# Two-layer decoder trunk: group norm, even units' scores and the mixed inputs of layer B placed anew between the products

## The chip, the cores and the metric

One core of one Trainium2 chip runs the kernel. The metric is the device time of one execution in microseconds (us), taken as the median of several runs.

## The reference

One inference step of a trunk of two layers, for a prompt of 256 tokens (with 16 meta tokens ahead, 272 positions) and 8 samples of one token. All is fp32. Layer A is RWKV-7 time mixing, layer B grouped-query attention over a window of 128 with sinks. Cut to what matters here:

```python
def rwkv7_step(S, inp):
    r, d, k, v, kk, b = inp
    sa = jnp.einsum('bhij,bhj->bhi', S, kk)
    S = S * d[:, :, None, :] - sa[..., None] * b[:, :, None, :] + v[..., None] * k[:, :, None, :]
    return S, jnp.einsum('bhij,bhj->bhi', S, r)
...
    rkvz = jnp.einsum('btpd,pde->btpe', xm[:, :, :4], w_rkvz)
...
    S_fin, y = lax.scan(rwkv7_step, S0.astype(f32), ...)
    y = (y - mean) * lax.rsqrt(var + GN_EPS) * gn_g + gn_b
    y = y + jnp.sum(r_h * k_h * r_k, axis=-1, keepdims=True) * v_h
    y = y.reshape(B, T, WIDTH) * jax.nn.silu(z)
    return y @ w_out, S_fin, xn[:, -1]
```

After layer A one shared key/value product `w_kv` is taken of the stream, and layer B's products `w_qz` and `w_o` follow. The weights of layer A's four input products have 2048 x 4096 entries each, `w_out` 4096 x 2048, `w_kv` 2048 x 1024.

## The kernel before

**Products.** Each fp32 weight tile is split into a high and a low half (`split`, L192: ACT casts `whi` at L195, DVE subtracts to `wlo` at L197), and each product is three matmuls per tile (`mm3`, L218 high by high, L219 high by low, L220 low by high) over 280 columns (the 272 positions and the 8 samples). `products()` cuts them into pieces of six such matmuls, and `self.pos` counts pieces.

**The recurrence between them.** `phase_a` calls `drive` (L608), which goes through the pieces in order. Ahead of each piece it lets a list of streams (Python generators) put in their small work, and each stream says with its `yield` for how many pieces it then sleeps and, if it likes, for which condition. PE runs all of this in the order in which it is written. The heads of layer A are worked in 16 units of 4 heads, `u`, two units to a call `o`:

- `prep(u)` makes the unit's inputs: two small gate products (`ps_l`), then a DMA that spreads the norms of the keys into `kk`, and on DVE the key times its norm (L898), two scans (L910) and more.
- `scores(u)` multiplies keys and queries inside chunks of 64 positions, in five steps: three groups of matmuls (`ps_sc`, L1017 and L1031; DVE reads them at L1024, L1025, L1037 and L1038, ACT at L1023 and L1036) and two groups of transposes (`ps_bk`). For an even unit every step takes both banks of the PSUM pool `pe`, which has two. The gaps between its steps are 8, 6, 6, 5, 4 pieces.
- `substitute(o)` inverts the triangles of 16 on DVE: a transpose to `NL` (L1069), 14 pairs of small operations (L1075, L1077), transposes to `TN` (L1081) and `TR` (L1082). `solve(o)` goes on with four groups of small matmuls on PE (`ps_so`, L1102, L1108, L1120, L1129), the first of them 24 or 27 pieces after the scores.
- `chain(o)` walks over five chunks: W (L1191), two pieces later X (L1205, L1208), three later G (L1214, L1217), five later the next W. It is written in `main()`, whose work has a higher priority in the scheduler of the other engines' instructions.
- `group_norm(o)` (L1255) normalises the result, 36 pieces later transposes it back in four groups of three transposes (L1275, `ps_yt`), three pieces apart, two groups to one double bank, and adds each to the bonus `vT` on DVE (L1276).
- `bo` (L954) is the product that makes the bonus, `vk` (L854) a copy on ACT of transposed values.

**Layer B's inputs.** Once the stream is done, `out_a` starts the `w_kv` product (`ps_kv`). `phase_b` then makes the 16 mixed inputs `bmx` of `w_qz` with `norm_mix`, an ACT operation (L1464, `bmh`) and a DVE operation (L1465, `bml`) each, all 16 written at one place.

## Time and profile before

| | us |
|---|---|
| median of 3 runs | 2120.92 |
| lowest, highest run | 2119.35, 2124.57 |
| the profiled execution | 2118.32 |
| its span in the trace | 2116.5 |
| PE busy in it | 2064.9 (98%) |
| DVE busy | 1697.8 (80%) |
| ACT busy | 1263.8 (60%) |
| the 16 DMA engines, mean busy share | 66.6% |

The profiled execution is 1.8 us longer than its span, and 2.6 us below the median of the runs. Busy times are of the span. The start of a PE row is the time from which to read (the ends of matmuls are modelled, and one overlaps the next), and PEclk is the share of full clock that TensorE was granted.

### The profile page before, as it was taken

Reading aid. Unit: us, or ns where it says so; the run is one execution under the profiler, and the core shown is the slowest. Engines: PE = TensorE matmul, PEld = TensorE weight load, DVE = VectorE, ACT = ScalarE, POOL = GpSimd, SP = SyncE. Lnnn points to the kernel's source line nnn. Section 1 sums busy time; section 2 is a strip of 40 time slices with the busy share of each in tenths; the row PEclk is TensorE's granted clock in tenths of the full one; section 3 lists DMA queues with packets and bytes.
Section 4 is the critical chain, followed back from the end, with each engine's and each line's share of the span. In section 5 each row is a group of like instructions: output and inputs, shape, how many; then the busy total and the mean of one; then the engine's idle time right before and its main releaser. Section 6 shows DMA issues by size and latency. Waiting matters only on the chain.

```text
span 2116.5 us, 55871 instructions
## 1 busy us (share of the span) xinstructions
PE 2064.9 (98%) x21420; PEld 1965.8 (93%) x21420; DVE 1697.8 (80%) x4112; ACT 1263.8 (60%) x2790; POOL 122.5 (6%) x188
## 2 busy tenths in 40 slices
PE   9999999899999999999999999999999999999997
PEld 7999899889899989899999999999999999999997
DVE  8867777687678878888888788997888888878885
ACT  3457766576766757767676445565565655544443
POOL 0011100001010010100100001100000000000000
PEclk9999999999999999999999999999999999999999
DMA  7898667658756876777657687757455444567774
GB/s 258 314 312 250 189 213 241 188 181 290 216 180 205 260 229 198 211 217 222 203 152 246 207 257 243 247 172 227 132 167 156 146 155 130 181 210 247 232 219 132
DMA packets 276356, 446.28 MB, mean 211 GB/s; under 512 B 54056, under 2 KB 97768, under 8 KB 275696
## 3 DMA queue, kind: packets, MB, share of 16 engines
q1 hardware_dynamic: 275656, 441.66, 66.6%
q8 instruction: 168, 2.75, 0.5%
q10 hardware_dynamic: 432, 1.05, 0.1%
q14 instruction: 100, 0.82, 0.1%
HBM read 381.69 MB, written 65.03 MB: 211 GB/s over the span
## 4 chain that ended last, share of the span: by engine, by line
PE 87%; DVE 5%; ACT 3%; DMA 3%; issue 2%; SPq 0%; POOL 0%; DVEq 0%; POOLq 0%; ACTq 0%
PE ps_z L218 6%; PE ps_z L219 6%; PE ps_z L220 6%; PE ps_k L218 3%; PE ps_ob L218 3%; PE ps_ob L220 3%; PE ps_v L218 3%; PE ps_ob L219 3%; PE ps_r L218 3%; PE ps_q L218 3%; PE ps_q L220 3%; PE ps_q L219 3%; PE ps_k L219 3%; PE ps_k L220 3%; PE ps_v L220 3%; PE ps_v L219 3%
## 5 line engine op out<-in xcount | busy, mean ns | idle before, releaser
L218 PE MATMUL ps_z<-mhlm,whi_z 128*128 128x280 f32 x512 | 158.6, 310 | 2.8 <-ACT sr L937 2.0
L219 PE MATMUL ps_z<-mhlm,whi_z 128*128 128x280 f32 x512 | 150.6, 294 | 0.0
L220 PE MATMUL ps_z<-mhlm,wlo_z 128*128 128x280 f32 x512 | 150.3, 294 | 0.0
L218 PE MATMUL ps_q<-bmh,whi_qb 128*128 128x264 f32 x512 | 150.0, 293 | 0.1
L218 PE MATMUL ps_z<-bmh,whi_zb 128*128 128x264 f32 x512 | 147.4, 288 | 0.0
L220 PE MATMUL ps_q<-bmh,wlo_qb 128*128 128x264 f32 x512 | 145.6, 284 | 0.6 <-DVE wlo_qb L197 0.6
L219 PE MATMUL ps_q<-bml,whi_qb 128*128 128x264 f32 x512 | 145.6, 284 | 0.0
L219 PE MATMUL ps_z<-bml,whi_zb 128*128 128x264 f32 x512 | 145.5, 284 | 0.0
L220 PE MATMUL ps_z<-bmh,wlo_zb 128*128 128x264 f32 x512 | 145.4, 284 | 0.0
L218 PE MATMUL ps_ob<-ghi,whi_ob 128*128 128x264 f32 x512 | 145.3, 285 | 0.0
L220 PE MATMUL ps_ob<-ghi,wlo_ob 128*128 128x264 f32 x512 | 144.6, 284 | 0.0
L219 PE MATMUL ps_ob<-glo,whi_ob 128*128 128x264 f32 x512 | 144.6, 283 | 0.0
L195 ACT CAST whi_ob<-raw_ob 128x512 fp32r<-128x512 f32 x128 | 79.1, 620 | 96.9 <-PE ps_ob L219 77.8
L195 ACT CAST whi_oa<-raw_oa 128x512 fp32r<-128x512 f32 x128 | 79.2, 620 | 88.0 <-PE ps_oa L219 30.6
L197 DVE TENSOR_TENSOR wlo_r<-raw_r,whi_r 128x512 fp32r<-128x512 f32 x128 | 87.8, 691 | 42.6 <-ACT whi_r L195 41.3
L218 PE MATMUL ps_v<-mhlm,whi_v 128*128 128x280 f32 x384 | 119.8, 312 | 0.4 <-ACT st L790 0.4
L218 PE MATMUL ps_k<-mhlm,whi_k 128*128 128x280 f32 x384 | 119.1, 310 | 1.0 <-ACT st L790 1.0
L195 ACT CAST whi_v<-raw_v 128x512 fp32r<-128x512 f32 x128 | 79.0, 619 | 65.8 <-PE ps_v L219 37.7
L197 DVE TENSOR_TENSOR wlo_v<-raw_v,whi_v 128x512 fp32r<-128x512 f32 x128 | 87.3, 687 | 36.9 <-ACT whi_v L195 35.6
L195 ACT CAST whi_zb<-raw_zb 128x512 fp32r<-128x512 f32 x128 | 78.2, 619 | 62.9 <-PE ps_z L219 38.5
L220 PE MATMUL ps_k<-mhlm,wlo_k 128*128 128x280 f32 x384 | 112.4, 293 | 2.1 <-issue 2.1
L219 PE MATMUL ps_v<-mhlm,whi_v 128*128 128x280 f32 x384 | 112.7, 293 | 0.0
(478 smaller groups left out, 7604.1 us busy)
## 6 DMA issues: line engine op xcount, KB each, us to landing
raw_k<-a_w_rkvz SPq DMA_DIRECT2D x128, 256.0 KB
raw_v<-a_w_rkvz SPq DMA_DIRECT2D x128, 256.0 KB
raw_r<-a_w_rkvz SPq DMA_DIRECT2D x128, 256.0 KB
raw_z<-a_w_rkvz SPq DMA_DIRECT2D x128, 256.0 KB
raw_oa<-a_w_out SPq DMA_DIRECT2D x128, 256.0 KB
raw_qb<-b_w_qz SPq DMA_DIRECT2D x128, 256.0 KB
raw_zb<-b_w_qz SPq DMA_DIRECT2D x128, 256.0 KB
raw_ob<-b_w_o SPq DMA_DIRECT2D x128, 256.0 KB
```

Of the source, the lines that this page charges most:

```text
L195: self.nc.scalar.copy(hi, src)
L197: return self.nc.vector.tensor_tensor(lo, src, hi.bitcast(F32), op=ALU.subtract)
L218: mm(ps, wh, xh, start=start, stop=False)
L219: mm(ps, wh, xl, start=False, stop=False)
L220: return mm(ps, wl, xh, start=False, stop=stop)
```

## The change

1. `drive` takes `main` ahead of the epilogues in each piece, and notes in `self.ran` the piece in which `main` stepped. `near(n)` is a condition that holds when `main` stepped in this same piece, or n pieces after it was set.
2. The five steps of an even unit's scores sleep 7, 5, 5, 5, 5 pieces, and from unit 2 on they wait besides for `near(n + 3)`: they come in the piece in which the chain (or another part of `main`) has a step, behind it on PE, or three pieces later.
3. Unit 4's `prep` sleeps 7 pieces between the DMA to `kk` and the DVE operation on it.
4. The first group of `solve` waits 24, 29, 24, 24, 24, 27, 31, 27 pieces in calls 0 to 7 (before: 24 in calls 0 to 4 and 27 in 5 to 7).
5. `group_norm` transposes in two groups of six, each in a double bank of its own, six pieces apart.
6. `bmx[k]` is issued behind the cast of the weight unit 7 + k of the `w_kv` product.
7. The streams of layer B's `drive` change places (an idle one and `heads`).

```diff
@@ -192,7 +192,7 @@
     def split(self, hi, lo, src):
 
         with self.tc.issue_after(self.root) if self.hold else contextlib.nullcontext():
-            self.nc.scalar.copy(hi, src)
+            self.cast = self.nc.scalar.copy(hi, src)
         with self.tc.issue_after(self.hold) if self.hold else contextlib.nullcontext():
             return self.nc.vector.tensor_tensor(lo, src, hi.bitcast(F32), op=ALU.subtract)
 
@@ -211,6 +211,7 @@
             self.raws.append(nc.sync.dma_start(raw.rearrange("p k c -> p (k c)"), w[col // 256, k0 // 2]))
             hi, lo = t("whi", F32R), t("wlo", F32R)
             self.los.append(self.split(hi, lo, raw))
+            self.casts.append(self.cast)
             yield k0, hi, lo
 
     def mm3(self, ps, wh, wl, xh, xl, start, stop):
@@ -601,14 +602,14 @@
         self.pad_v(0)
         self.pad_v(1)
 
-        self.drive(self.products(), [self.epilogues(), self.main(), preps, self.decodes(), self.late_gates(), self.keep_r()],
+        self.drive(self.products(), [self.main(), self.epilogues(), preps, self.decodes(), self.late_gates(), self.keep_r()],
                    {preps: [wait, need]})
 
 
 
 
     def drive(self, products, streams, begun, ahead=2000):
-        self.samples = False
+        self.samples, self.ran = False, -1
         live = [[g, *begun.get(g, (0, None))] for g in streams]
 
         now = streams[:2]
@@ -620,8 +621,10 @@
 
                         turn = self.tc.issue_after(self.los[-2].ins) if self.pos and s[0] not in now else \
                             contextlib.nullcontext()
+                        if s[0] is now[0]:
+                            self.ran = self.pos
                         try:
-                            with self.tc.high_priority(offset=ahead if s[0] is now[1] else 0), turn:
+                            with self.tc.high_priority(offset=ahead if s[0] is now[0] else 0), turn:
                                 w = next(s[0])
                         except StopIteration:
                             live.remove(s)
@@ -639,6 +642,11 @@
     def after(self, n, *ks):
 
         return lambda: all(k in self.done and self.pos >= self.done[k] + n for k in ks)
+
+    def near(self, n):
+
+        due = self.pos + n
+        return lambda: self.ran == self.pos or self.pos >= due
 
     def pp_bank(self, name):
         self.pp_pos = self.pos
@@ -894,6 +902,8 @@
 
         kk = w("kk")
         self.spread(kk, self.kr[u // 4][4 * u % 16:4 * u % 16 + 4])
+        if u == 4:
+            yield 7
         for j in range(2):
             V.scalar_tensor_tensor(kk[:, j], kT[:, j], self.pcol(P_KK, p0 + j), kk[:, j], op0=MU, op1=MU)
 
@@ -985,7 +995,7 @@
         nc, rp = self.nc, self.rp
 
         odd = u % 2
-        gap = iter((8, 3, 4, 3, 3) if odd else (8, 6, 6, 5, 4))
+        gap = iter((8, 3, 4, 3, 3) if odd else ((n, self.near(n + 3) if u else None) for n in (7, 5, 5, 5, 5)))
         turn = iter((0, odd, 0, odd, 0))
         def banks(nm):
             if next(turn):
@@ -1094,7 +1104,7 @@
         ev = lambda n, *s: rp.tile([128, 512], F32, tag="ev", bufs=2, name=f"{n}{o}")[:, :s[0] * s[1]].rearrange(
             "p (i t) -> p i t", t=s[1])
 
-        yield 24 if o < 5 else 27
+        yield (24, 29, 24, 24, 24, 27, 31, 27)[o]
         ps = self.bank(self.pe, f"ps_so{o}")
         Q = [slice(32 * q, 32 * q + 32) for q in range(4)]
         for i in range(16):
@@ -1264,18 +1274,19 @@
         V.tensor_scalar(var, var, 1.0 / 64, GN_EPS, op0=MU, op1=AD)
         self.rsqrt(var, rp, "y", o)
         V.tensor_tensor(y, y, bc(var), op=MU)
-        for j in range(4):
-            u = 2 * o + j // 2
+        for i in range(2):
+            u = 2 * o + i
             b = self.U[u]['bonus']
-            yield 3 if j else 36 if o < NU // 2 - 1 else 19
-            if j % 2 == 0:
-                two = self.two_banks(f"ps_yt{o}_{j}")
-            ps = two[:, j % 2]
-            for c in range(3):
-                nc.tensor.transpose(ps[:, 128 * c:128 * c + 128], Y[:, c, j].rearrange("p q i -> p (q i)"), self.ident)
-            V.scalar_tensor_tensor(b[:, j % 2, :L], ps[:, :L], self.pcol(P_GG, 4 * o + j), b[:, j % 2, :L],
-                                   op0=MU, op1=AD)
-            if j % 2 and o < GZ // 2:
+            yield 6 if i else 36 if o < NU // 2 - 1 else 19
+            two = self.two_banks(f"ps_yt{o}_{i}")
+            for k in range(2):
+                for c in range(3):
+                    nc.tensor.transpose(two[:, k, 128 * c:128 * c + 128], Y[:, c, 2 * i + k].rearrange("p q i -> p (q i)"),
+                                        self.ident)
+            for k in range(2):
+                V.scalar_tensor_tensor(b[:, k, :L], two[:, k, :L], self.pcol(P_GG, 4 * o + 2 * i + k), b[:, k, :L],
+                                       op0=MU, op1=AD)
+            if o < GZ // 2:
                 nc.sync.dma_start(self.yd[u // 2][:, 2 * (u % 2):2 * (u % 2) + 2, :L], b[:, :, :L])
         self.mark('g', o)
 
@@ -1451,6 +1462,7 @@
             if k >= KT - 2:
                 nc.tensor.matmul(pst[:, :N], ones, acc if k == KT - 2 else sq, start=k == KT - 2,
                                  stop=k == KT - 1)
+        self.kv0 = len(self.casts)
         units = self.wunits(self.I['w_kv'][0], "kv", KT, 0, 256, 2)
         self.kvu = itertools.chain([next(units) for _ in range(5)], units)
         nc.scalar.activation(self.rb, pst[:, :N], AF.Ln, bias=self.epst, scale=1.0 / D)
@@ -1533,7 +1545,10 @@
             dma(f('p_cache_v')[0], self.Vd)
             dma(f('s_cache_k')[:, WIN - 1], ksn)
             dma(O['s_cache_v'][:, WIN - 1], self.Vn[0:64:8, :, 0])
-            self.bmx = [self.norm_mix(bp, "bm", P_BN, k) for k in range(KT)]
+            self.bmx = []
+            for k in range(KT):
+                with self.tc.issue_after(self.casts[self.kv0 + 7 + k].ins):
+                    self.bmx.append(self.norm_mix(bp, "bm", P_BN, k))
         self.wx = None
         self.close("wx0", "st0", "kv")
         right = dict(side="right", reuse_waits="tile")
@@ -1561,7 +1576,7 @@
         def idle():
             while True:
                 yield 1 << 20
-        self.drive(self.products_b(), [idle(), self.heads(), self.gates_b()], {}, 0)
+        self.drive(self.products_b(), [self.heads(), idle(), self.gates_b()], {}, 0)
 
     def products_b(self):
 
```

Three places show how the order of the instructions moves.

**DVE, between the end of call 1's triangles and the group norm of call 0** (`NL1`, `TN1`, `TR1`: the triangles of call 1; `kk4`, `kT4`, `cl4`, `ta4`: unit 4's `prep`; `vT0`, `vT1`: the bonus of units 0 and 1; `ps_yt0_0`: the transposed result of unit 0). Before:

```order
L898 SCALAR_TENSOR_TENSOR kk4_5449<-kT4_5445,par_79,kk4_5449 128x280
L1075 TENSOR_TENSOR stmp1_14_5118<-NL1_5077 128x28
L898 SCALAR_TENSOR_TENSOR kk4_5449<-kT4_5445,par_79,kk4_5449 128x280
L910 SCALAR_TENSOR_TENSOR cl4_4871<-reset_1751,cl4_4871 128x272 x2
L904 TENSOR_TENSOR kT4_5445<-kT4_5445,km0_4_5454 128x280
L1077 TENSOR_TENSOR NL1_5077<-NL1_5077,stmp1_14_5118 128x2x14
L197 TENSOR_TENSOR wlo_v_1280_14_5425<-raw_v_1280_14_5422,whi_v_1280_14_5424 128x512
L904 TENSOR_TENSOR kT4_5445<-kT4_5445,km1_4_5457 128x280
L906 TENSOR_TENSOR ta4_4872<-ta4_4872,kk4_5449 128x560
L1081 STREAM_TRANSPOSE TN1_5123<-NL1_5077 128x512
L1082 STREAM_TRANSPOSE TR1_5124<-NL1_5077 128x512
L1276 SCALAR_TENSOR_TENSOR vT0_2043<-ps_yt0_0_5399,par_79,vT0_2043 128x272
```

With the change:

```order
L1085 TENSOR_TENSOR stmp1_14_5118<-NL1_5077 128x28
L1087 TENSOR_TENSOR NL1_5077<-NL1_5077,stmp1_14_5118 128x2x14
L1091 STREAM_TRANSPOSE TN1_5123<-NL1_5077 128x512
L1092 STREAM_TRANSPOSE TR1_5124<-NL1_5077 128x512
L197 TENSOR_TENSOR wlo_v_1280_14_5430<-raw_v_1280_14_5427,whi_v_1280_14_5429 128x512
L1287 SCALAR_TENSOR_TENSOR vT0_2043<-ps_yt0_0_5399,par_79,vT0_2043 128x272 x2
L197 TENSOR_TENSOR wlo_v_1536_0_5455<-raw_v_1536_0_5452,whi_v_1536_0_5454 128x512
L197 TENSOR_TENSOR wlo_v_1536_2_5483<-raw_v_1536_2_5480,whi_v_1536_2_5482 128x512
L197 TENSOR_TENSOR wlo_v_1536_4_5508<-raw_v_1536_4_5505,whi_v_1536_4_5507 128x512
L908 SCALAR_TENSOR_TENSOR kk4_5449<-kT4_5445,par_79,kk4_5449 128x280 x2
```

The first operation on `kk4` stood ahead of `TN1`, `TR1` and `vT0`, and now stands behind them and behind three weight halves more; the two operations on `vT0` stand together, behind one pair of transposing groups.

**PE, the third step of the recurrence of call 2 and the second score group of unit 6** (`ps_ch2_1`: the chain's chunk 1; `ps_sc02_6`, `ps_sc12_6`: the scores; `ps_k_2816`: the product that runs). Before:

```order
L1191 MATMUL ps_ch2_1_8552<-X0_2_7154,E_5_7139 64x64 x2
L218 MATMUL ps_k_2816_1_8452<-mhlm1_19_2_7303,whi_k_2816_4_8455 128x280
L219 MATMUL ps_k_2816_1_8452<-mhlm1_19_2_7303,whi_k_2816_4_8455 128x280
L220 MATMUL ps_k_2816_1_8452<-mhlm1_19_2_7303,wlo_k_2816_4_8456 128x280
L218 MATMUL ps_k_2816_1_8452<-mhlm1_19_2_7303,whi_k_2816_4_8455 128x280
L219 MATMUL ps_k_2816_1_8452<-mhlm1_19_2_7303,whi_k_2816_4_8455 128x280
L220 MATMUL ps_k_2816_1_8452<-mhlm1_19_2_7303,wlo_k_2816_4_8456 128x280
L1017 MATMUL ps_sc12_6_8575<-E_6_8138,KB_1739 128x128
L1017 MATMUL ps_sc02_6_8574<-E_6_8138,KB_1739 128x128
```

With the change:

```order
L1201 MATMUL ps_ch2_1_8498<-X0_2_7144,E_4_6068 64x64 x2
L1201 MATMUL ps_ch2_1_8498<-X0_2_7144,E_5_7123 64x64 x2
L1027 MATMUL ps_sc12_6_8539<-E_6_8186,KB_1739 128x128
L1027 MATMUL ps_sc02_6_8538<-E_6_8186,KB_1739 128x128
...
L1027 MATMUL ps_sc12_6_8539<-E_6_8186,KB_1739 128x128
L1027 MATMUL ps_sc02_6_8538<-E_6_8186,KB_1739 128x128
L219 MATMUL ps_k_2816_0_8451<-mhlm1_19_2_7323,whi_k_2816_4_8455 128x280
L220 MATMUL ps_k_2816_0_8451<-mhlm1_19_2_7323,whi_k_2816_4_8455 128x280
L221 MATMUL ps_k_2816_0_8451<-mhlm1_19_2_7323,wlo_k_2816_4_8456 128x280
```

A whole piece of six product matmuls lay between the chain's group and the scores; now the scores follow the chain directly, and the products go on behind both.

**ACT, in the `w_kv` product** (`whi_kv`: casts of its weights; `bmh`: the mixed inputs of layer B; `rb`: the root of the mean square). Before:

```order
L1464 ACTIVATE bmh8_22749<-hT_20526,par_79 128x280
L1457 ACT_TABLE_LOAD
L1457 ACTIVATE rb_20527<-rb_20527 128x280
L1464 ACTIVATE bmh9_22753<-hT_20526,par_79 128x280
L1464 ACTIVATE bmh10_22757<-hT_20526,par_79 128x280
L1464 ACTIVATE bmh11_22761<-hT_20526,par_79 128x280
L1464 ACTIVATE bmh12_22765<-hT_20526,par_79 128x280
L195 CAST whi_kv_0_14_22101<-raw_kv_0_14_22099 128x512
L195 CAST whi_kv_256_0_22166<-raw_kv_256_0_22164 128x512
L1464 ACTIVATE bmh13_22769<-hT_20526,par_79 128x280
```

With the change:

```order
L1469 ACTIVATE rb_20527<-rb_20527 128x280
L195 CAST whi_kv_0_14_22101<-raw_kv_0_14_22099 128x512
L1476 ACTIVATE bmh0_22717<-hT_20526,par_79 128x280
L195 CAST whi_kv_256_0_22166<-raw_kv_256_0_22164 128x512
L1476 ACTIVATE bmh1_22721<-hT_20526,par_79 128x280
L195 CAST whi_kv_256_2_22172<-raw_kv_256_2_22170 128x512
L1476 ACTIVATE bmh2_22725<-hT_20526,par_79 128x280
L195 CAST whi_kv_256_4_22202<-raw_kv_256_4_22200 128x512
```

The casts of `whi_kv_0_14` and `whi_kv_256_0` stood behind 13 of the `bmh`; now each `bmh` stands behind one cast.

## Rows read from the trace of the kernel before

**Rows 1.** The page: busy time, share of the span and instructions of each engine.
```profile
PE 2064.9 (98%) x21420; PEld 1965.8 (93%) x21420; DVE 1697.8 (80%) x4112; ACT 1263.8 (60%) x2790; POOL 122.5 (6%) x188
```

**Rows 2.** Waits of PE over the span: what for, us in total, times, longest us.
```profile
PE ps_yt L1275 <- DVE vT L1276: 8.0, 2, 6.9
PE ps_so L1102 <- DVE TN L1081: 6.1, 2, 3.5
...
PE ps_bo L954 <- ACT vk L854: 2.0, 1, 2.0
...
PE ps_kv L218 <- ACT whi_kv L195: 1.8, 1, 1.8
```

**Rows 3.** Timeline of PE (start us, us, engine, line, what, [idle before]): a score group.
```profile
611.86 0.29 PE L220 MATMUL ps_r<-mhlm,wlo_r 128*128 128x280 f32 x1
612.08 1.16 PE L1017 MATMUL ps_sc<-E,KB 64*128 64x128 f32 x16
613.17 0.40 PE L218 MATMUL ps_r<-mhlm,whi_r 128*128 128x280 f32 x1
613.40 0.29 PE L219 MATMUL ps_r<-mhlm,whi_r 128*128 128x280 f32 x1
```

**Rows 4.** Timeline of PE, 639 us: products behind a transposing group (the column order as above).
```profile
639.65 0.37 PE L218 MATMUL ps_r<-mhlm,whi_r 128*128 128x280 f32 x1
639.87 0.29 PE L219 MATMUL ps_r<-mhlm,whi_r 128*128 128x280 f32 x1
```

**Rows 5.** Timeline of PE, 375 to 382 us: the second transposes of ps_yt0_0.
```profile
381.96 0.90 PE L1275 MATMUL ps_yt<-consts,Y 128*128 128x128 f32 x3 [6.92 <-DVE vT L1276]
```

**Rows 6.** Timeline of DVE, 375 to 382 us.
```profile
375.65 0.51 DVE L898 SCALAR_TENSOR_TENSOR kk<-kT,par,kk 128x280 f32<-128x280 f32 x1 [4.24 <-DMA kk<-kr]
...
381.45 0.46 DVE L1276 SCALAR_TENSOR_TENSOR vT<-ps_yt,par,vT 128x272 f32<-128x272 f32 x1
```

**Rows 7.** Windows: us, PE busy (count), PEld, DVE, ACT, POOL, PEclk (granted clock), DMA share, GB/s.
```profile
382.00:388.00 6.00, 6.00 (x30) 5.99 (x31) 2.66 (x6) 3.82 (x6) 0.00 (x0) 0.57 0.55 175
916.00:920.00 4.00, 4.00 (x20) 3.96 (x19) 0.86 (x2) 1.87 (x4) 0.20 (x1) 0.54 0.75 244
862.00:865.00 3.00, 2.83 (x22) 2.83 (x23) 2.56 (x6) 2.98 (x7) 0.00 (x0) 1.00 0.66 212
1390.60:1394.20 3.60, 3.60 (x17) 3.60 (x17) 3.60 (x11) 2.77 (x6) 0.00 (x0) 0.53 0.59 212
1394.20:1428.00 33.80, 33.72 (x264) 33.24 (x263) 33.23 (x75) 16.83 (x37) 1.10 (x2) 1.00 0.57 171
```

**Rows 8.** Timeline of DVE, 884 to 914 us: the fifth solve, first and last transpose.
```profile
884.73 1.10 DVE L1069 STREAM_TRANSPOSE NL<-N 128x512 f32<-128x512 f32 x1 [0.77 <-POOL N L1066]
...
912.25 1.04 DVE L1081 STREAM_TRANSPOSE TN<-NL 128x512 f32<-128x512 f32 x1
```

**Rows 9.** Timeline of PE: first matmuls of the solves of calls 0 and 5.
```profile
256.24 1.27 PE L1102 MATMUL ps_so<-TN,Noff 32*32 32x16 f32 x128 [3.50 <-DVE TN L1081]
...
913.43 1.90 PE L1102 MATMUL ps_so<-TN,Noff 32*32 32x16 f32 x128 [2.56 <-DVE TN L1081]
```

**Rows 10.** Timeline of PE, 862 and 898 us.
```profile
862.17 0.39 PE L954 MATMUL ps_bo<-rklhi,ones 128*128 128x272 f32 x1 [2.03 <-ACT vk L854]
...
898.81 0.55 PE L1275 MATMUL ps_yt<-consts,Y 128*128 128x128 f32 x3 [1.06 <-DVE vT L1276]
```

**Rows 11.** Timeline of ACT, 1381 to 1386 us.
```profile
1381.70 3.88 ACT L1464 ACTIVATE bmh<-hT,par 128x280 fp32r<-128x280 f32 x9
```

**Rows 12.** Windows of the kv product (columns as in rows 7).
```profile
1380.00:1388.00 8.00, 7.80 (x60) 7.48 (x58) 4.98 (x12) 7.70 (x15) 0.00 (x0) 1.00 0.50 161
...
1396.00:1404.00 8.00, 8.00 (x65) 7.98 (x64) 7.96 (x17) 4.60 (x9) 0.00 (x0) 1.00 0.73 216
```

**Rows 13.** Timeline of PE, 1072 us: the product behind the first score group of unit 14.
```profile
1072.43 0.40 PE L218 MATMUL ps_z<-mhlm,whi_z 128*128 128x280 f32 x1
```

**Rows 14.** Timeline of DVE, 1077 us: the last read of that score group.
```profile
1077.40 0.43 DVE L1025 TENSOR_TENSOR E<-ps_sc,consts 128x256 f32<-128x256 f32 x1
```

More of the change, by code (lines that the diff above doesn't have):

```diff
@@ L112, in __init__ @@
         self.nc, self.tc, self.I, self.O = nc, tc, I, O
-        self.raws, self.los = [], []
+        self.raws, self.los, self.casts = [], [], []
         self.wx = self.hold = None
```

## The prediction

> **What bounds the kernel now.** I read the page's busy times first. PE is busy for 98% of the span, DVE for 80% and ACT for 60% [rows 1], so the time is the length of PE's queue plus the holes in it. The change adds and removes no work: the counts of instructions stay. It can win only in two ways: shorter passages between two kinds of PE work, and holes that close. The second view is the list of PE's waits. All of them come to some 40 us, spread over two dozen places; the rows show the four that the change touches [rows 2]. The third view is the timeline around each hole, with the windows for the granted clock.
>
> A passage costs something because products and fp32 groups don't follow each other smoothly. Two products start 0.128 us apart (33.80 us for 264) [rows 7]. From the last product to a score group it is 0.22 us, and from the first product behind the group to the second 0.23 us [rows 3]: 0.09 and 0.10 above the pace, 0.19 in all. Behind a transposing group only the second passage is slow, 0.22 us, 0.09 too much [rows 4].
>
> A hole can cost more than itself. Behind the hole of 6.92 us [rows 5] the granted clock is 0.57 in the window from 382 to 388 us, so mostly at the lower of the two levels (1.2 of 2.4 GHz), and 30 PE instructions take 6.00 us where the pace gives 30 x 0.128 = 3.8 [rows 7]. Behind 2.56 us (913 us) and 1.8 us (the `w_kv` product) it is 0.54 and 0.53; behind 2.03 us (862 us) it stayed at 1.00 [rows 2, 7, 9, 10].
>
> **The change part by part.**
>
> *Scores behind the chain, six transposes at a time.* The order counts 421 separate stretches of small work on PE before and 386 with the change: 24 score or `bk` groups more stand directly at a chain group, 13 separate transposing groups fewer remain, and two groups that touched now stand apart. 24 x 0.19 + 13 x 0.09 - 2 x 0.19 = 5.4 us less. Bounds: half of that, should passages from chain to scores cost as much as one to a product, and 35 x 0.19 = 6.7.
>
> *Unit 4's wait, with the merged group norm.* The second three transposes of `ps_yt0_0` waited 6.92 us [rows 5] for the DVE operation that reads the first three, which started at 381.45 [rows 6]. DVE works in order: it stood 4.24 us at `kk`'s first operation, which waits for a DMA, and then had scans and the three transposes of the solve ahead of `vT0` [rows 6]. With the change, the operations on `kk4` stand behind `vT0`, and the six transposes need no read between them. What is late next is the second group, six pieces (36 x 0.128 = 4.6 us) after the first; the operations left ahead of `vT0` are two small ones, two transposes and one weight half, some 3 us. So the hole goes, and with it the slow stretch: 6.9 + (6.0 - 3.8) = 9.1 us. The DMA has the seven pieces (5.4 us) to land, against the 4.24 us that DVE stood there.
>
> *The fifth solve.* PE waited 2.56 us for `TN`, its matmuls took 1.90 us where the same 128 take 1.27 at full clock [rows 9], and the 20 instructions from 916 to 920 us took 4.00 instead of 2.6 [rows 7]: 2.6 + 0.6 + 1.4 = 4.6 us. From DVE's first transpose to the last of this solve 27.5 us pass [rows 8], filled with 72 operations of 27.1 us. By the order 55 of them with 19.0 us of work are left in the same 33 pieces, since unit 10's scores and its follow-up work have moved ahead by 7 to 9 pieces. `TN` then is some 8 us earlier and PE doesn't wait: -4.6, or nothing at worst. The first solve, with its 3.50 us [rows 9], keeps its 65 operations; I leave it standing.
>
> *Two smaller holes.* `bo1` of unit 11 stood 2.03 us behind an ACT copy for another unit [rows 2, 10]; it now comes 15 pieces earlier, ahead of that copy: -2.0 (or 0). The three transposes at 898.81 waited 1.06 us for the read of the three ahead [rows 10]; merged, they don't: -1.1 (or 0).
>
> *The mixed inputs.* `whi_kv` was late by 1.8 us [rows 2], behind nine `bmh` in a row (3.88 us) and four more [rows 11], and the slow clock then made 17 instructions take 3.60 us instead of 2.2 [rows 7]: 3.2 us in all. One `bmh` per cast ends this wait. But DVE is busy 7.96 of 8 us right behind it [rows 12], the same splits and the same 16 `bml` are still to be made, and the weight buffers let it run ahead by five units only. What DVE left idle from 1380 to 1388 us, 3.0 us [rows 12], can't all be used. I take -0.5, nearer to the DVE row than to the ACT row; bounds -3.2 and 0.
>
> *New waits.* Even units' steps now come five pieces after one another, and each takes both banks of `pe`. So a step waits until the step before has been read out; it stands in PE's queue, and the products behind it wait too. The tightest case is unit 14: the group ends by 1072.43 [rows 13], its last read ends at 1077.40 + 0.43 = 1077.83 [rows 14], 5.4 us later, and the next step would be due 4.8 us after the group. Worked out like this for the 28 gaps of seven units, the slack runs from -0.5 to 5.3 us, 2.5 in the mean: 0.5 us of waits if reads stay as they are, 4.2 if each comes 1 us later. I take 2.0.
>
> *At nothing.* The later first groups of two solves (calls 1 and 6) delay only the chain: the chain's last step is at piece 1066 instead of 1068, and products go on beyond it. If that cover were gone, five pieces would cost 3.9 us. `main` ahead of the epilogues swaps neighbours inside a piece, and layer B's order doesn't move.
>
> **Sum.** -5.4 - 9.1 - 4.6 - 2.0 - 1.1 - 0.5 + 2.0 = -20.7 us. The profiled execution took 2118.3, so 2097.6; the median of the runs shown stands 2.6 above it, which gives **2100 us**.
>
> **The rivals.**
>
> *A, the forecast*: most of the holes close, 2100. With every unknown at its better end (no new wait, the `w_kv` hole gone, 35 full passages, the first solve's wait too) it is 2100 - 2.0 - 2.7 - 1.3 - 3.5 = 2090.5. With the fifth solve, unit 11's bonus, the passages at half and the new waits at 4.2 it is 2100 + 4.6 + 2.0 + 2.7 + 2.2 = 2111.5.
>
> *B, the big hole only moves*: DVE's scans and `kk4` run into the next thing that PE needs (the second transposing group, or the first matmuls of the solve, which are 5 pieces later). For it: the work is the same, and the DMA's margin is 5.4 - 4.24 = 1.2 us. Against: nothing in PE's queue needs unit 4's `prep` for 20 pieces. The 9.1 us stay: 2109.
>
> *C, the stream doesn't get faster*: PE, freed of its holes, meets weights that aren't split or loaded yet. For it: DVE at 80%, and near 100% in the `w_kv` product. Against: in the list of waits no hole of over 1 us names a weight half of layer A, and the DMA engines are busy 55 to 75% in the windows read [rows 7]. Only the passages would be left, 2118.3 - 5.4 + 2.6 = 2115.5, up to no change, 2121.
>
> *D, slower: bank waits at most steps.* Place: the 35 steps of the even units. Price: if scores and the chain, now issued together, delay each other's reads on DVE and ACT by 3 us, the 28 slacks leave 27 us of waits, seven of them of at least 1.8 us with a slow stretch of 1.4 us behind: 37 us against 22.7 won, 2118.3 + 14.3 + 2.6 = 2135. It decides from about 2.6 us of delay on. Against: DVE and ACT do the same work, and `main` keeps its priority. The Trainium skill, page "TensorE: Matmul & The Clock Gate", section "A second HAM failure mode: psum-queue depth-cycling", tells of a kernel that went through PSUM banks in turn, whose PE paused so often between groups that its clock swung between the two levels and throughput fell. By that rule this change invites D. The trace here speaks half for it: the clock fell behind a pause of 1.8 us, and not behind one of 2.03.
>
> **How the numbers follow.** A 0.73, B 0.13, C 0.09, D 0.05. A measurement tells 0.3% (6.4 us) from no change, so A and B count as faster (0.86), C as the same (0.09), D as slower (0.05). The range holds A with both its ends and B, and leaves out C and D: 2090 to 2113.
>
> **What the profile would show.** Right: no wait of over 1 us at `ps_yt` or at the fifth `ps_so`, the granted clock at 1.00 from 372 to 390 us and around 910 us, no wait of `ps_bo` for `vk`, and short waits of `ps_sc` or `ps_bk` for L1024 to L1038's reads at units 12 and 14. Wrong: `ps_yt` or `ps_so1` still behind DVE by several us (B); a list of waits with `wlo` or `whi` in front (C); many waits of `ps_sc` and `ps_bk` and new windows at the low clock (D). A `w_kv` hole that vanishes whole would put the time at the lower half of A.

## The result, and the profile after

The changed kernel takes 2125.86 us (median of 11 runs, 2121.47 to 2129.17), the kernel before on the same chip 2119.45 (11 runs, 2115.30 to 2124.57). The ratio is 1.0025, with a 95% interval of 1.0015 to 1.0034: slower by 6.4 us, where 20.7 less were forecast. The profiled execution took 2124.85 us with a span of 2123.1; that of before had 2116.5.

The page after, busy time by engine:

```profile
PE 2063.7 (97%) x21420; PEld 1965.2 (93%) x21420; DVE 1699.6 (80%) x4112; ACT 1262.4 (59%) x2790; POOL 120.7 (6%) x188
```

Work is the same as before [rows 1]: PE is busy 1.2 us less, in a span 6.6 us longer. So the loss is idle time on PE. The list of PE's waits after (what for, us in total, times, longest us) answers to [rows 2]:

```profile
PE ps_l L219 <- ACT cl L891: 3.7, 3, 2.3
PE ps_ch L1201 <- DVE X L1237: 3.6, 4, 1.3
PE ps_so L1118 <- issue: 3.5, 3, 1.8
PE ps_so L1112 <- DVE TN L1091: 3.5, 1, 3.5
PE ps_ch L1201 <- ACT X L1237: 3.1, 3, 2.3
PE ps_l L219 <- ACT ta L891: 2.8, 2, 2.1
PE ps_bk L1059 <- DVE E L1035: 2.4, 1, 2.4
PE ps_z L219 <- issue: 2.2, 1, 2.2
PE ps_kv L221 <- DVE wlo_kv L197: 2.2, 4, 0.8
PE ps_r L219 <- ACT st L798: 2.0, 1, 2.0
PE ps_so L1130 <- DVE TN L1125: 1.8, 1, 1.8
...
PE ps_kv L219 <- DVE rout_k L1706: 1.7, 1, 1.7
```

What the forecast wanted closed is closed: no line names `ps_yt`, `ps_bo` no longer waits for `vk`, and of the two waits of `ps_so` for the first `TN` only the first solve's is left. But the list has new heads. `ps_l` (the small decay and gate products of a unit's `prep`), `ps_ch` (the chain) and `ps_bk` wait for ACT and DVE. No line names `ps_sc`, whose bank waits the forecast had priced at 2.0 us.

Two stretches, by windows (columns as in [rows 7]), first that of the big hole, then one behind a new hole:

```profile
382.00:388.00 6.00, 5.89 (x164) 5.66 (x165) 6.00 (x13) 4.88 (x15) 4.28 (x3) 1.00 0.98 334
...
808.00:812.00 4.00, 4.00 (x38) 3.50 (x38) 4.00 (x11) 3.97 (x12) 0.90 (x2) 0.57 0.28 70
```

From 382 to 388 us the granted clock is 1.00 where it was 0.57, as forecast. From 808 to 812 us it is 0.57, behind a pause that the kernel before did not have.

**Where the time went.** Take PE's instructions in both traces, give each one as its pace the median distance from the one ahead of it, among all instructions of the same line and shape with the same two kinds ahead, and call what goes beyond it a hole:

| | before | after |
|---|---|---|
| first to last start on PE | 2103.8 | 2110.4 |
| at the pace of each kind | 2029.7 | 2025.5 |
| holes over 0.6 us | 35.9 | 45.0 |
| shorter ones | 38.2 | 39.9 |

(An instruction at the lower clock counts here as a short hole.) The better order brings 4.2 us, and holes give back 9.1 + 1.7 = 10.8. How pace and shorter holes share the time hangs on how finely kinds are told apart (by one instruction ahead instead of two, the order brings 0.9); the holes over 0.6 us don't. A second reading goes by place. The products are issued in pieces of six matmuls, numbered alike in both kernels; the start of a piece after, less the same piece's start before, tells how far the changed kernel is ahead (negative) or behind:

| piece | 325 | 375 | 450 | 550 | 575 | 675 | 700 | 800 | 850 | 1250 | 1275 | 1300 to the end |
|---|---|---|---|---|---|---|---|---|---|---|---|---|
| after less before, us | -9.1 | -10.3 | -8.4 | -3.9 | -6.5 | -5.6 | +0.6 | +1.5 | +7.2 | +5.6 | +1.9 | +6.7 |

At piece 325 the big hole has closed and the gain is there in full. It is then spent in steps, most of them at holes that are new: holes over 0.6 us come to 34.6 us after at places where the kernel before has none (the same tile within eight pieces), and 22.8 us of the old ones are gone.

**One new hole, followed back.** The one at piece 687 (807 us) took 2.3 us. PE's timeline (columns as in [rows 3]):

```profile
804.50 0.29 PE L221 MATMUL ps_v<-mhlm,wlo_v 128*128 128x280 f32 x1
807.06 0.39 PE L219 MATMUL ps_l<-lt5h,lhi 96*128 96x280 f32 x1 [2.28 <-ACT cl L891]
```

The bank of `ps_l` is read by `cl`'s tanh on ACT. ACT:

```profile
803.50 0.41 ACT L1237 COPY X<-FS 64x256 f32<-64x256 f32 x1 [4.81 <-DVE FS L1233]
803.81 0.74 ACT L1239 COPY Y<-ps_ch 64x256 f32<-64x256 f32 x2
804.56 1.29 ACT L1033 COPY F<-ps_sc 32x256 f32<-32x256 f32 x4
805.87 0.62 ACT L195 CAST whi_v<-raw_v 128x512 fp32r<-128x512 f32 x1
806.52 0.49 ACT L891 ACTIVATE cl<-ps_l,par 128x280 f32<-128x280 f32 x1
```

ACT stood 4.81 us at a copy for the chain, with seven operations more between it and the tanh. It waited for `FS`, on DVE:

```profile
799.71 0.69 DVE L1324 TENSOR_TENSOR dT<-dS,ve 128x512 f32<-128x512 f32 x1 [2.12 <-DMA dS<-state_wkv]
...
802.37 0.68 DVE L1325 TENSOR_REDUCE dy<-dT 128x8 f32<-128x512 f32 x1
802.96 0.17 DVE L296 TENSOR_SCALAR rsyk<-kx 128x35 int32<-128x35 int32 x1
803.05 0.41 DVE L1233 TENSOR_TENSOR FS<-ps_ch,PC 128x256 f32<-128x256 f32 x1
```

DVE stood 2.12 us at an operation of the decode step whose transfer had not landed, with `FS` six operations behind. Here each engine took its operations in the order of its queue, so one late transfer stopped three. The change edits none of these lines. Of what they do it moves the scores (the copies of `F`, 1.29 us) and, by one piece, this call's chain. In the kernel before DVE reached the same `dT` at 797.65 us without a wait.

The queues of DVE and ACT are laid out by a scheduler, which places operations by its own idea of times. Comparing the orders gives 538 places on DVE and 403 on ACT (a place is a run of rows that stands in one order and not so in the other) where before and after differ, over all of layer A and not only around the edits. The forecast quoted the three places that it had looked for.

### The profile page after: what moved, and what is told of

Read it like the earlier page. It is cut to its first block, busy times and chain, and to the rows that moved or that the text cites. A ratio compares the mean times of both kernels' runs of the same rounds, so it can differ in the third digit from the quotient of the medians.

```text
span 2123.1 us, 55869 instructions
## 1 busy us (share of the span) xinstructions
PE 2063.7 (97%) x21420; PEld 1965.2 (93%) x21420; DVE 1699.6 (80%) x4112; ACT 1262.4 (59%) x2790; POOL 120.7 (6%) x188
## 4 chain that ended last, share of the span: by engine, by line
PE 84%; DVE 6%; DMA 4%; ACT 3%; issue 2%; SPq 0%; POOL 0%; DVEq 0%; POOLq 0%; ACTq 0%
PE ps_z L219 5%; PE ps_z L220 5%; PE ps_z L221 5%; PE ps_k L219 3%; PE ps_r L219 3%; PE ps_ob L219 3%; PE ps_ob L221 3%; PE ps_ob L220 3%; PE ps_v L219 3%; PE ps_q L219 3%; PE ps_k L220 3%; PE ps_q L221 3%; PE ps_q L220 3%; PE ps_r L220 3%; PE ps_r L221 3%; PE ps_k L221 3%
## 5 line engine op out<-in xcount | busy, mean ns | idle before, releaser
L219 PE MATMUL ps_v<-mhlm,whi_v 128*128 128x280 f32 x384 | 118.8, 309 | 1.1 <-ACT st L798 1.1
L221 PE MATMUL ps_v<-mhlm,wlo_v 128*128 128x280 f32 x384 | 111.6, 291 | 1.1 <-issue 1.1
L197 DVE TENSOR_TENSOR wlo_ob<-raw_ob,whi_ob 128x512 fp32r<-128x512 f32 x128 | 87.2, 691 | 31.3 <-ACT whi_ob L195 29.1
```

What stands on the lines that cost most here:

```text
L197: return self.nc.vector.tensor_tensor(lo, src, hi.bitcast(F32), op=ALU.subtract)
L219: mm(ps, wh, xh, start=start, stop=False)
L221: return mm(ps, wl, xh, start=False, stop=stop)
```

## The experiments

Two theories stand first. One: a part of the change (the scores' new place, the group norm, `main` ahead of the epilogues) makes the loss. The rival: any edit has the queues of DVE and ACT laid anew behind it, and the new layout falls better or worse. Ratios are to the kernel before on the same chip.

**Parts taken out of the change, or made alone**

Even units' scores at the old gaps, the rest of the change kept:

```diff
-        gap = iter((8, 3, 4, 3, 3) if odd else ((n, self.near(n + 3) if u else None) for n in (7, 5, 5, 5, 5)))
+        gap = iter((8, 3, 4, 3, 3) if odd else (8, 6, 6, 5, 4))
```

> The changed kernel with the even units' scores at their old gaps (8, 6, 6, 5, 4) and no wait for the chain's step; all other parts stay. Theory 1 (the scores' new places make the new holes: their reads on ACT and DVE meet the chain's, and the wait of ps_l, ps_bk and of the chain's W follows): the holes that the other parts closed stay closed and the new ones go, 2119.5 - 9.1 - 2.0 - 1.1 - 3 = about 2104 us (2098 to 2110). Theory 2 (the order of this program is a draw: any rearrangement closes some holes and opens others of the same sum): 2116 to 2128, with new holes at other places. Theory 3 (main ahead of the epilogues makes the new holes): as the changed kernel, 2122 to 2128.

2128.14 us, 1.0036 [1.0024, 1.0049]. The holes at pieces 588, 800, 811, 855 and 938 are there without the new scores, and three pieces behind 687 there is one of 2.1 us, at `ps_ch`. The loss doesn't need the scores' new place.

The scores' new gaps alone, on the kernel before (the same line, with `near` and `ran`):

> The kernel before with the change of the even units' scores alone (gaps 7, 5, 5, 5, 5 and the wait for the chain's step). Theory 1: the passages saved (24 x 0.19 = 4.6 us) and new holes of some 18 us, 2119.5 + 13 = about 2132 us (2127 to 2138), with holes at ps_l behind ACT, and ps_yt's 6.9 us still there. Theory 2: 2114 to 2128. Theory 3: the passages alone are saved, 2115 us.

2125.13 us, 1.0016 [1.0005, 1.0026]. The big hole stays (8.6 us). Holes over 0.6 us come to 43.1 us, 7.2 more than before. So this part alone makes new holes too, at other places than the whole change does; 1.7 us of them are waits of `ps_sc`, the kind that the forecast looked for.

Merged group norm and unit 4's wait alone, on the kernel before:

```diff
+        if u == 4:
+            yield 7
...
+            yield 6 if i else 36 if o < NU // 2 - 1 else 19
+            two = self.two_banks(f"ps_yt{o}_{i}")
```

> The kernel before with the merged transposes of the group norm and unit 4's wait of 7 pieces alone. Theories 1 and 3: the hole of 6.9 us at 382 us goes with its slow clock (9.1 us) and the 1.1 us at 899, and nothing new opens: 2119.5 - 10 - 1 = about 2108 us (2104 to 2112). Theory 2: the hole goes and others open, 2114 to 2122.

2121.07 us, 1.0008 [0.9995, 1.0022]. The big hole goes, with 7.4 us of lead at piece 325. By piece 800 the kernel is 1.4 us behind. Two holes of before have grown, at 529 us (1.5 to 3.2 us) and at 915 us (2.6 to 3.6), and one of 3.3 us at 807 us is new, behind the same `dS` transfer. DVE's order differs from before in 367 places.

`main` behind the epilogues again, the rest kept:

```diff
-        self.drive(self.products(), [self.main(), self.epilogues(), preps, self.decodes(), self.late_gates(), self.keep_r()],
+        self.drive(self.products(), [self.epilogues(), self.main(), preps, self.decodes(), self.late_gates(), self.keep_r()],
```

> The changed kernel with the epilogues ahead of main again. Theory 1: little, 2122 to 2129. Theory 3: products no longer wait for ACT's st copies, and the new holes go with them: 2104 to 2115 us. Theory 2: anywhere from 2116 to 2130, with the holes at other places.

2125.24 us, 1.0014 [1.0002, 1.0026], with the holes of the whole change. It swaps 43 places and costs nothing, as forecast.

Unit 4's wait alone, on the kernel before (the two lines above):

> The kernel before with one edit: unit 4's wait of 7 pieces between the DMA to kk and its use. DVE's order of before and of this kernel differs at 299 places, the first at the edit, the others all the way to the end of layer A. Theory 2 (the scheduler lays the queues of DVE and ACT anew behind any edit, and the holes there are drawn anew): the 6.9 us at 382 go, the holes from 400 us on stand at other places, and the sum is 2114 to 2126. Theory 4 (the merged transposes of the group norm open the new holes from 550 us on): this kernel keeps its gain, 2119.5 - 9.1 = about 2111 us (2108 to 2113).

2117.71 us, 1.0005 [0.9996, 1.0015]. The lead is 8.3 us at piece 325 and 2.1 in the end.

The merged group norm alone, on the kernel before:

> The kernel before with the merged transposes of the group norm alone. Theory 4: the new holes without unit 4's gain, 2124 to 2130 (the hole at 382 us in part still there). Theory 2: 2114 to 2128, the holes at other places than in the run with both edits.

2138.52 us, 1.0100 [1.0082, 1.0117]. `ps_yt` still waits 5.3 us, for the read behind `kk4`: merging alone doesn't close the big hole, the order on DVE does. Its list of waits has new holes besides: 5.1 us of `ps_ch` behind `X`, 3.1 of `ps_sm`, 4.0 of `ps_v` and `ps_r` behind `st`.

**Edits that should be worth nothing in themselves**

The rival says that an edit with no worth of its own moves the time as much. The second solve one piece later, on the kernel before:

```diff
-        yield 24 if o < 5 else 27
+        yield (24, 25, 24, 24, 24, 27, 27, 27)[o]
```

> The kernel before with an edit that is worth nothing by itself: the first group of the second solve one piece later (25 instead of 24). DVE's order changes at 412 places from there on. Theory 2: the holes from 560 us on change places, by several us each, and the time moves by up to 8 us, slower more likely than faster. Theory 4, and any theory by which the order behind the edit is worth the same: 2117 to 2122, with the holes of before (781, 862, 899, 913, 1048 us) in place.

2137.46 us, 1.0096 [1.0075, 1.0118]. One piece (0.8 us) of delay of one group costs 19.5 us; DVE's order has 412 new places. Waits of PE in this kernel, in its fastest execution (2129.44 us, with 11.1 of the 19.5 us):

```profile
PE ps_yt L1275 <- DVE vT L1276: 8.5, 2, 7.8
PE ps_ch L1205 <- ACT W L1196: 4.3, 3, 2.0
...
PE ps_ch L1191 <- DVE X L1227: 3.6, 3, 1.6
PE ps_ch L1205 <- ACT W L1200: 2.8, 2, 2.5
PE ps_sm L935 <- POOL sm L932: 2.8, 1, 2.8
```

The same kind of hole as after the change, from one number. This number is in the change too, which makes the second solve wait 29 pieces. Six more of this kind, each with one number of the solves' or the group norm's delay changed by one, on either kernel (the column "places" counts DVE's against its parent):

| edit | parent | places | median us | ratio |
|---|---|---|---|---|
| group norm of call 0: 36 to 37 | before | 13 | 2116.09 | 0.9989 [0.9977, 1.0001] |
| third solve: 24 to 25 | before | 221 | 2121.83 | 1.0012 [1.0002, 1.0022] |
| third solve: 24 to 25 | after | 452 | 2121.97 | 1.0008 [0.9998, 1.0018] |
| fifth solve: 24 to 25 | after | 316 | 2115.50 | 0.9980 [0.9970, 0.9990] |
| second solve: 29 to 30 | after | 81 | 2121.33 | 1.0006 [0.9991, 1.0021] |
| fifth solve: 24 to 25 | before | 108 | 2124.35 | 1.0022 [1.0010, 1.0035] |

In their order:

> The kernel before with the first group norm's transposes one piece later (37 instead of 36 pieces, call 0 alone). DVE's order changes at 13 places only. Theory 2 (the order of the queues makes the holes, and few places move few holes): the second half of layer A keeps its holes (781, 862, 913, 1048 us of before), 2115 to 2123. Theory 7 (the program is at the edge of something that any delay in calls 0 and 1 tips over, whatever the order): as with the second solve one piece later, 2130 to 2140.

> The kernel before with the first group of the third solve one piece later (25 instead of 24, call 2 alone); DVE's order changes at 221 places from there on. Theory 2: holes behind 550 us change places, 2116 to 2138, slower more likely, since the order before is a kept one. Theory 7: nothing happens in calls 0 and 1, so 2117 to 2122.

> The changed kernel with the same edit, the first group of the third solve one piece later (25 instead of 24); DVE's order changes at 452 places. Theory 2: the holes from 560 us on are drawn anew, on either side of the changed kernel: 2112 to 2138. If the parts of the change keep a worth of their own beneath the draw, such draws lie below those of the kernel before with the same kind of edit (2137). Any theory by which the changed kernel's holes belong to one of its parts: 2122 to 2130, with the holes at pieces 588, 687, 800 and 855 in place.

> The changed kernel with the first group of the fifth solve one piece later (25 instead of 24); DVE's order changes at 316 places from piece 660 on. Theory 2: the holes up to 780 us stay, those behind are drawn anew, 2115 to 2136. A theory by which the holes belong to one part: 2122 to 2130, with the holes at pieces 687, 800 and 855 in place.

> The changed kernel with the first group of the second solve one piece later (30 instead of 29): the edit that cost the kernel before 19 us. DVE's order changes at 81 places. Theory 2: few places, so near the changed kernel, 2118 to 2132. If the edit cost by itself (a later solve): 2140 to 2147.

> The kernel before with the first group of the fifth solve one piece later (25 instead of 24): the edit that gave the changed kernel 10 us. DVE's order changes at 108 places, all behind 780 us. Theory 2: the holes up to 780 us stay, the others are drawn anew, 2114 to 2130. If the edit is worth something by itself: 2107 to 2111.

(In this part solves are counted from one: "fifth" is call 4. The prediction's and [rows 8]'s fifth solve is that of call 5.) The edit with 13 places kept the holes of before at their pieces, and that with 81 kept most of after's; those with hundreds closed some and opened others. A kind of edit has no fixed worth: a second solve one piece later costs 19.5 us on before (24 to 25) and nothing on after (29 to 30); a fifth solve one piece later gains some 10 us on after and loses 4 on before. The changed kernel with a later fifth solve is the fastest measured, and beats both kernels. Its DVE (columns as above), where the hole at 807 us was:

```profile
795.78 0.69 DVE L1324 TENSOR_TENSOR dT<-dS,ve 128x512 f32<-128x512 f32 x1 [0.67 <-DMA dS<-state_wkv]
...
799.29 0.42 DVE L1233 TENSOR_TENSOR FS<-ps_ch,PC 128x256 f32<-128x256 f32 x1
799.62 0.17 DVE L296 TENSOR_SCALAR rsyk<-kx 128x35 int32<-128x35 int32 x1
```

The wait for `dS` is 0.67 us and `FS` stands ahead of `kx`; PE has no hole at `ps_l` there. The changed kernel's closed big hole is kept, and this profiled execution is 7.0 us ahead of before's (the medians are 3.3 apart).

Two local gains together, on the changed kernel (fifth solve 25, and the first solve 28 pieces, which removes its wait of 3.5 us):

```diff
-        yield (24, 29, 24, 24, 24, 27, 31, 27)[o]
+        yield (28, 29, 24, 24, 25, 27, 31, 27)[o]
```

> The changed kernel with the fifth solve one piece later (the fastest so far) and the first group of the first solve 4 pieces later (28 instead of 24), so that its wait of 3.6 us at 256 us goes with its slow clock (4.9 us in all). DVE's order changes at 599 places from there on. If local gains add up: 2115.5 - 4.9 = about 2110.5. Theory 2: the hole at 256 us goes, and the rest is drawn anew: 2112 to 2136.

2121.60 us, 1.0003 [0.9988, 1.0019]. The first solve's hole falls from 3.6 to 0.6 us, and yet by the ratios the two together are some 5 us worse than the fifth solve's edit alone (the intervals just touch): a hole of 3.0 us opens at 395 us, and two grow, at 377 us (0.9 to 2.2) and at 908 us (2.7 to 3.9).

**Do the transfers set the pace?** If layer A waited for its transfers, whatever the order, work added to PE ahead of the new holes would shrink them. The group norm of call 0 repeats its first six transposes 21 times (the result is the same):

```diff
-                for c in range(3):
+                for c in (0, 1, 2) * (21 if o == 0 and i == 0 else 1):
```

> The changed kernel with 120 transposes more on PE at the first group norm (the same six done 21 times over, 9.4 us of PE work by 0.078 us each), where the change had won its 9 us. Orders of DVE differ at 87 places from the changed kernel's. Theory 5 (something else, such as transfers, sets the pace from 500 to 1000 us, and any lead is lost there): the delay is taken up, 2124 to 2129. Theories 2 and 4: it comes on top, 2126 + 9 = 2135 (2131 to 2139).

2132.45 us, 1.0080 [1.0065, 1.0095]. 120 transposes more, 9.4 us of PE's time, came out as 6.6 us more than after by the medians and 11.7 by the ratios (0.0055 x 2119), and the holes at 588, 687, 800 and 855 stayed. So most of the delay adds to the time, and the transfers don't set the pace of layer A as a whole. But the trace, of the fastest of the six runs (2127.84 us), has some of the delay taken up: this kernel is 11.3 us behind after at piece 325, 5.5 at piece 500, where after's holes at 334, 447 and 498 are gone, and 3.0 at the end. That something like a transfer limits this stretch isn't ruled out.

**The chain of one hole, broken link by link.** The changed kernel with the late `dS` operation seven pieces later:

```diff
-            yield 5 if g < 3 else 4, lambda: self.samples
+            yield 12 if (g, q) == (1, 6) else 5 if g < 3 else 4, lambda: self.samples
```

> The changed kernel with 12 pieces instead of 5 between the transfer of one block of the samples' states (group 1, block 6) and its use. In the changed kernel DVE waits 2.1 us for this transfer at 800 us with four operations on the block and then the chain's first read (FS of call 4) behind it; here the block's operations stand behind that read, and DVE's order differs at 72 places in all. If the wait at DVE's head makes the hole: the hole of 2.4 us at piece 687 (ps_l behind ACT's cl, 807 us) goes with its slow clock (about 1.3 us), the holes ahead of it stay. If the scores' reads on ACT make it (four copies of F stand there too): it stays, 2 us or more. The time: 2120 to 2128, since what follows may be drawn anew.

2136.24 us, 1.0075 [1.0058, 1.0092]. The hole stays, 2.15 us. DVE now stands at the next transfer in its queue:

```profile
803.19 0.18 DVE L296 TENSOR_SCALAR rsyk<-kx 128x35 int32<-128x35 int32 x1 [2.69 <-DMA kx<-kr]
```

The kernel as a whole is 10 us slower than after. Its profiled execution lost 7.0 us at one place of layer B that the edit does not touch (piece 1330, where PE waits 4.53 us for DVE's `q`); the runs don't say why.

Then the operations on `kx` moved too (the load stays, the operations come 13 pieces later, behind a weight half), with and without the edit on `dS`:

```diff
-            self.key_norms(p0 // 8)
+            if p0 // 8 == 3:
+                x, d = self.key_load(3)
+                yield 13
+                with self.tc.issue_after(self.los[-2].ins):
+                    self.key_store(3, x, d)
```

> The changed kernel with both operations that wait for a transfer taken from ahead of the chain's first read of call 4 on DVE: the block of the samples' states (12 pieces instead of 5 after its transfer) and the key norms of group 3 (13 pieces after theirs). Ahead of the read stand only weight halves now; DVE's order differs at 24 places. If transfers at DVE's head make the hole at piece 687: FS of call 4 starts before 801 us instead of 803, ACT's copy of X follows, and the hole of 2.4 us goes to under 0.5, with its slow clock. If not: 2 us or more stay. The time, with few places moved: 2126 - 3.5 = about 2122 (2116 to 2128).

> The changed kernel with the key norms alone moved behind the chain's first read of call 4; the block of the samples' states still stands ahead of it on DVE and waits for its transfer. DVE's order differs at 25 places. If each of the two waits alone is enough: the hole at piece 687 stays at 1.5 to 2.4 us. If kx is what matters: it goes to under 0.5. The time: 2120 to 2130.

With both moved, the hole is gone. `FS` on DVE, `X` on ACT and `ps_l` on PE:

```profile
800.17 0.42 DVE L1246 TENSOR_TENSOR FS<-ps_ch,PC 128x256 f32<-128x256 f32 x1 [0.65 <-PE ps_ch L1240]
...
800.63 0.41 ACT L1250 COPY X<-FS 64x256 f32<-64x256 f32 x1 [1.83 <-DVE FS L1246]
...
804.74 0.29 PE L219 MATMUL ps_l<-lt5h,lhi 96*128 96x280 f32 x1
```

`FS` now waits for PE, not the other way. With `kx` alone moved the hole shrinks from 2.28 to 0.44 us, but there PE came to the place 4.2 us later than after (piece 680), which by itself leaves ACT more time. With both moved PE came there within 0.1 us of after. So the reading of this hole is shown by that run: a transfer at the head of DVE's queue, and the chain's read behind it. The time did not follow: 2128.32 us, 1.0041 [1.0025, 1.0058] with both, 2126.02 us, 1.0030 [1.0019, 1.0042] with one. With both, 24 places changed on DVE, and eleven pieces later `ps_ch` waits 2.9 + 1.1 us where after had no hole.

## Why the prediction was wrong

**What held.** The bound was right: the time is PE's queue and its holes. Of the sum's terms:

- Passages, -5.4: -4.2 by the paces above, inside its bounds. This is an estimate, since it hangs on how kinds are told apart.
- Unit 4's wait and the group norm, -9.1: the hole is gone, and its clock with it. From piece 314, where the changed kernel is 1.1 us behind, to piece 325, where it is 9.1 ahead, it wins 10.2 us. It is unit 4's wait that does it (8.3 of lead alone), not the merged transposes (alone they leave 5.3 us of the hole).
- Unit 11's bonus, -2.0, and the transposes at 899 us, -1.1: both holes are gone (2.2 and 1.2 us beyond the pace).
- Mixed inputs, -0.5: the wait for `whi_kv` went whole (from piece 1250 to 1275 the changed kernel wins 3.7 us), but the product then waits for DVE (`wlo_kv` 2.2 us, `rout_k` 1.7), and 4.8 are lost up to piece 1300: +1.1. That DVE would be late next was said; it took more than the hole had cost.

**What was mis-sized.** *The fifth solve* (call 5), -4.6: the wait for `TN` went (2.56 us), but around the solve's next steps PE now waits 0.63 us for `ET`, then 2.23 us before `ps_z` and 1.79 for the second `TN` (922.05 us). The stretch at the lower clock there shrinks from 6.8 to 3.4 us. Taken together the gain is about nothing. The term asked whether `TN` comes in time and not what the operations behind it then wait for.

**The step that failed** is "New waits", +2.0. It looked for new waits only where the change issues something new, at the even units' score banks, and found them small; after the change the list has none over 0.3 us there (the one longer wait of `ps_bk`, 2.4 us, is an odd unit's, and is there with the old scores too). What came in the term's place is 34.6 us of new holes at other places (8.5 of them those of the fifth solve and the mixed inputs), partly made up by some 10 us of old ones that closed without having been named. Behind it stood an assumption that the prediction never wrote down: that the queues of DVE and ACT stay as they were beyond the edited places. They differ in 538 and 403 places. With the redrawn queues the holes over 0.6 us went from 35.9 to 45.0 us even though those named above had closed. Adding local gains as if the rest stood still was the error: in the experiments two local gains put together were no better than one of them.

**The rivals.** D had the right sign and the wrong mechanism: no wait of `ps_sc` after the change, and the loss is there with the old scores too. C's price, 2115.5 to 2121, was nearest to the time, but not for its reason: in layer A one product alone waited for a weight half (`whi_k`, 1.2 us). B did not happen. The prediction cites the Trainium skill (page "TensorE: Matmul & The Clock Gate", section "A second HAM failure mode: psum-queue depth-cycling") for a kernel whose frequent pauses between groups, as it cycled through PSUM banks, made the clock swing. No run here tests this, since the pauses at the even units' banks did not come. Between 10 and 2100 us the clock records have seven stretches at the lower level in either kernel, 34.1 us before and 27.3 after.

**What stays open.** That the redrawn order makes the holes is shown for the one at piece 687; for the others it is argued from the experiments, since no run holds the order of DVE and ACT while the change is made. One part of the change stands untested as a cause: no run puts the second and seventh solves back to 24 and 27 pieces, and one piece of the second solve alone cost 19.5 us on the kernel before. In the change's own trace the lead still holds at piece 375, behind that solve, so it costs nothing on the spot. Whether the change has a worth of its own under the drawing of the queues can't be told from these runs. Kernels on before's side lie from 2116 to 2138 us, those on the change's side from 2115.5 to 2136 (the one with added transposes left aside), and each is one draw. That one-piece edits move the time by -10 to +19.5 us is shown; that the kernel before is a good draw is only argued, from what edits of it did (of eight, five were clearly slower and none clearly faster). Nor do the runs say why the kernel with both moves, a hole less, spreads from 2120 to 2138 us.

## What to carry to other kernels

Where a scheduler lays out the queues, compare the whole order of every engine before forecasting: if an edit moves hundreds of places on engines that it doesn't touch, the sum of its local gains is a guess within the width of the draw, here some 10 to 20 us. Measure that width first with an edit that should be worth nothing, and judge a change by several such draws of each side, since then a one-number variation may move the time more than the change does (here 10 us against 6). To protect a long chain, keep operations that wait for a transfer out of the queue ahead of its reads: 2.12 us of DVE's wait became 4.81 on ACT and 2.28 on PE.

## What the runs showed of the hardware that was not expected

How long PE paused does not tell whether the granted clock falls. After a pause of 2.39 us at 1014 us it stayed at 1.00, as after 2.03 in [rows 10]; after 2.06 us at 945 us, and after one of 0.99 us in a later solve (1172.86 us), it fell to 0.50, the lower of the two levels. The pauses in the changed kernel (columns as in [rows 3]), and the windows behind them (columns as in [rows 7]):

```profile
944.91 0.47 PE L219 MATMUL ps_l<-lt5h,lhi 96*128 96x280 f32 x1 [2.06 <-ACT ta L891]
1014.12 0.53 PE L1059 MATMUL ps_bk<-consts,KB 64*128 64x64 f32 x10 [2.39 <-DVE E L1035]
1172.86 0.59 PE L1118 MATMUL ps_so<-TR,ET 32*16 32x16 f32 x50 [0.99 <-issue]
...
945.20:948.40 3.20, 3.20 (x27) 2.82 (x27) 2.20 (x4) 2.55 (x8) 0.00 (x0) 0.50 0.72 187
1014.20:1018.00 3.80, 3.80 (x41) 3.50 (x42) 3.79 (x6) 3.36 (x9) 2.12 (x3) 1.00 0.77 235
1173.80:1177.00 3.20, 3.20 (x16) 3.20 (x16) 2.31 (x6) 1.25 (x3) 0.00 (x0) 0.50 0.89 306
```

The wait at 1014 us (piece 855) shows it best, since it comes back in other kernels. It took 2.43 us with the old scores and 2.43 us with `dS` and `kx` moved; the windows behind it, in this order:

```profile
1010.30:1013.70 3.40, 3.40 (x39) 3.11 (x39) 3.36 (x6) 2.95 (x7) 2.14 (x3) 1.00 0.75 244
1016.90:1020.30 3.40, 3.40 (x17) 3.37 (x15) 3.40 (x5) 2.18 (x5) 1.75 (x3) 0.50 0.77 243
```

So the price of a slow stretch, which the prediction set behind pauses of at least 1.8 us, does not hang on the length of the pause alone.
